# Weight buffers laid at equal places modulo 512 bytes in a hybrid decoder block

## The chip, the cores and the metric

The kernel runs on one core of a Trainium2 chip. The metric is the device time of one execution in microseconds (us), as the median of several runs.

## What is computed

One layer of a decoder block with 256 tokens and D = 2048, all in float32. One projection of the input feeds three branches of width 1024 (gated linear attention A, sliding-window attention B, block attention C). Each branch is projected up to D, weighted by a sigmoid gate, and summed; an output projection, a residual and a LayerNorm follow. Cut to what matters:

```python
def _hybrid_layer(x, w_in, ..., w_branch, w_o, ln_g, ln_b):
    proj = x @ w_in                                  # 2048 x 15632
    ...                                              # ya, yb, yc: three attention branches, each gated
    up = jnp.einsum('bsnw,nwd->bsnd', ys, w_branch)  # 3 x (1024 x 2048)
    gates = jax.nn.sigmoid(mgate.reshape(B, S, N_BRANCH, D) + b_merge)
    merged = jnp.sum(gates * up, axis=2)
    out = merged @ w_o                               # 2048 x 2048
    return _layer_norm(DEEPNORM_ALPHA * x + out, ln_g, ln_b)
```

## The kernel before

**Weights in chunks.** `plan` lists the weight matrices as 324 chunks of 128 x 1024 values (1040 for `av`), in the order of their use (`seq`). `emit_chunk` handles one: SP loads it into a raw buffer (L129, pool `wraw`, four buffers), ACT rounds it to the high part (L130, pool `whi`, three buffers), and DVE subtracts to get the low part (L131, pool `wlo`, three buffers). The buffers of a pool are taken in turn, so chunk number i uses high and low buffer i mod 3. `next_chunk` keeps two chunks ahead of the products. The activations `xhl` (and `ya`, `yb`, `yc`, `mhl`) hold high and low parts too, 512 values per k.

**Two kinds of product.** `mm3` (260 chunks: `aq`, `ak`, `ag`, `bq`, `bkv`, `bg`, `mg`, `wb`, `cq`, `ck`, `cg`) takes the weights as the stationary operand. For each of two column tiles and four k it issues a pair of matmuls; the load of the next weights runs beside the matmul ahead of it:

```python
nc.tensor.matmul(ps, hi[:, k, c], rhs[:, k0 + k, :], ...)                # L236: 512 columns, high part
nc.tensor.matmul(ps[:, 0:S], lo[:, k, c], rhs[:, k0 + k, 0:S], ...)      # L238: 256 columns, low part
```

`nproj` with `nmm` (64 chunks: `av`, `cv`, `wo`) has the activations stationary and the weights moving, in three matmuls per k (L278 to L280).

**Order of the work.** Chunks 0 to 31 are `aq`, `ak` and `av`. Chunks 32 to 131 are `ag`, `bq`, `bkv`, `bg` and the first merge (`mg` and `wb`), with the jobs of branches A and B between them: `tick` issues one step of each job after a chunk's products, so small matmuls and transposes of a job stand between two chunks on TensorE. Chunks 132 to 195 are `cq`, `ck`, `cv` and `cg`, without jobs. Chunks 196 to 213 open the second merge, with the jobs of branch C between them; 214 to 291 are the rest of the second and third merges, without jobs; 292 to 323 are `wo`, and LayerNorm ends the kernel.

**Where the buffers lie.** Pools are laid out one after the other in each partition, in the order of their creation, after the scratch of POOL's own DMA descriptors and the constants. A high or low buffer of 1040 values takes 4160 bytes, 64 more than a multiple of 512, so that three buffers of a pool lie at three places modulo 512:

| Buffers of chunk i | low part, modulo 512 | high part, modulo 512 | moving activations |
|---|---|---|---|
| i mod 3 = 0 | 32 | 224 | 416 |
| i mod 3 = 1 | 160 | 352 | 416 |
| i mod 3 = 2 | 96 | 288 | 416 |

Below, a chunk is said to be of class 0, 1 or 2 by i mod 3.

Of the kernel before, what the change touches and what calls it, by code (L numbers as in the profile page):

```python
# [9 lines left out]
F32 = mybir.dt.float32  # L10
F32R = mybir.dt.float32r
# [6 lines left out]
P = 128  # L18
# [9 lines left out]
RANK = 16  # L28
NV = 260
KC = 4  # L30
NWARM = 8


@with_exitstack
def kernel(ctx: ExitStack, tc: tile.TileContext, xT: bass.AP, x: bass.AP, w_in: bass.AP,
                             w_up: bass.AP, gla_b: bass.AP, norm_g: bass.AP, sinks: bass.AP, b_merge: bass.AP,
                             w_branch: bass.AP, w_o: bass.AP, ln_g: bass.AP, ln_b: bass.AP, out: bass.AP):
    nc = tc.nc

    const = ctx.enter_context(tc.tile_pool(name="const", bufs=1))  # L40
    wraw = ctx.enter_context(tc.tile_pool(name="wraw", bufs=4))
    wlo = ctx.enter_context(tc.tile_pool(name="wlo", bufs=3))
    whi = ctx.enter_context(tc.tile_pool(name="whi", bufs=3))
    acts = ctx.enter_context(tc.tile_pool(name="acts", bufs=1))
    work = ctx.enter_context(tc.tile_pool(name="work", bufs=2))
    pp = ctx.enter_context(tc.tile_pool(name="pp", bufs=2, space=PSUM))
    pa = ctx.enter_context(tc.tile_pool(name="pa", bufs=4, space=PSUM))

    # The weight chunks in the order of their use; loads and splits run ahead of the products.
    seq = []  # L50

    def deep(cols):
# [53 lines left out]
    def emit_chunk():  # L106
        i = state["in"]
        state["in"] += 1
        src, row0, col0, cols, name = seq[i]
        kc = deep(cols)  # L110

        def shaped(t):
            return t.rearrange("p (k c) -> p k c", c=cols)
        raw = shaped(wraw.tile([P, KC * NV], F32, tag="wraw", name=f"w{name}")[:, :kc * cols])
        if name.startswith("wo4_"):
            if not last:
                last["h"] = acts.tile([P, KT, 256], F32R, tag="y", name="wlasth", bufs=2)
                last["l"] = acts.tile([P, KT, 256], F32R, tag="y", name="wlastl", bufs=2)
            k0 = KC * int(name[4:])
            hi, lo = last["h"][:, k0:k0 + KC, :], last["l"][:, k0:k0 + KC, :]  # L120
        else:
            hi = shaped(whi.tile([P, KC * NV], F32R, tag="whi", name=f"h{name}")[:, :kc * cols])
            lo = shaped(wlo.tile([P, KC * NV], F32R, tag="wlo", name=f"l{name}")[:, :kc * cols])
        view = src[row0:row0 + kc * P, col0:col0 + cols].rearrange("(k p) c -> p k c", p=P)
        cuts = [0, 1, 2] if i < 2 else [0, kc]
        for a, b in zip(cuts, cuts[1:]):
            if name.startswith("aq_"):
                load_x(row0 // P + a, row0 // P + b)
            nc.sync.dma_start(raw[:, a:b, :], view[:, a:b, :])  # L129
            nc.scalar.copy(hi[:, a:b, :], raw[:, a:b, :])  # L130
            nc.vector.tensor_tensor(lo[:, a:b, :], raw[:, a:b, :], hi[:, a:b, :].bitcast(F32), op=ALU.subtract)  # L131
        ready.append((name, hi, lo))
# [6 lines left out]
        state["out"] += 1  # L139
        return hi, lo  # L140

    # Side work, cut in steps; one step of each running job is issued between two chunks.
    jobs = []

    def tick():
# [12 lines left out]
    xhl = acts.tile([P, KT, 2 * S], F32R, tag="x", name="xhl")  # L158
    xst = acts.tile([P, KT, S], F32, tag="y", name="xst", bufs=2)

    # The tensor engine's clock rises only while it is busy: keep it so until the first operands are there.
    wz = const.tile([P, 512], mybir.dt.bfloat16, name="wz")
    nc.vector.memset(wz, 0.0)
    pw = pa.tile([P, 512], F32, tag="pa", name="pw")
# [8 lines left out]
    nc.gpsimd.tensor_copy(ones, onesf)  # L173
    onerow = const.tile([P, 1], F32, name="onerow")
    nc.gpsimd.memset(onerow, 1.0)
    # The low-rank gate's weights three times over the rows (high, low, high parts), zeros between.
    wup3 = work.tile([96, 512], F32, tag="r", name="wup3")
    nc.gpsimd.memset(wup3, 0.0)
    for i in range(3):
# [23 lines left out]
    for i in (0, 2):  # L203
        nc.gpsimd.affine_select(mska[:, i, :], mska[:, i, :], pattern=[[-1, P]], compare_op=ALU.is_ge,
                                fill=NEG, base=0, channel_multiplier=1)
    # [row, column]: 1 where column > row; where column >= row; where column < row
    trif = work.tile([P, P], F32, tag="q1", name="trif", bufs=4)
    tril = const.tile([P, P], F32, name="tril")
    triu = const.tile([P, P], F32, name="triu")
# [98 lines left out]
    for k in range(0, KT, 2):  # L308
        hi, lo = next_chunk(f"aq_{k // 2}")
# [16 lines left out]
    def gla_job():  # L326
# [15 lines left out]
            return hl  # L342

        def sums(hl, name):
            # Sums over the partitions, the same in each row.
            pd = pa.tile([P, 512], F32, tag="pa", name=f"pd{name}")
            for e in range(2):
                nc.tensor.matmul(pd, ones, hl[:, e, :], start=e == 0, stop=e == 1)
            return pd
# [165 lines left out]
    def keys_job():  # L515
        nc.gpsimd.dma_start(ksw[0:64, :], bkv[64:128, 0, :])
        nc.gpsimd.dma_start(ksw[64:128, :], bkv[0:64, 0, :])
        yield from wait(2)
        # A key tile's values as [low parts | high parts]
        pv = pa.tile([P, 2, 2, 64], F32, tag="pa", name="pvb")  # L520
        for t in range(2):
            nc.tensor.transpose(pv[:, t, :, :], bkv[:, 1, t * P:(t + 1) * P], ident)
        nc.scalar.copy(vz[:, :, :, 64:P], pv)
        nc.vector.tensor_tensor(vz[:, :, :, 0:64], pv, vz[:, :, :, 64:P].bitcast(F32), op=ALU.subtract)
        yield from wait(2)
        for g in range(2):
            for r in range(2):
                rows = slice(64 * r, 64 * r + 64)
                src = bkv[rows, 0, :] if g == r else ksw[rows, :]
                nc.scalar.copy(ks[rows, g, 0, :], src)  # L530
                nc.vector.tensor_tensor(ks[rows, g, 1, :], src, ks[rows, g, 0, :].bitcast(F32), op=ALU.subtract)
# [1 line left out]
    yb = acts.tile([P, 8, 2 * S], F32R, tag="y", name="yb", bufs=2)  # L533

    def swa_job(hp):
        # A head's queries stand over its 64 rows as their high and low parts: products with the keys' high
        # parts twice and low parts twice give all four terms.
        g = hp // 4
        c0 = 1024 + 512 * (hp % 2)
        qs = swaw[:, c0:c0 + 512].rearrange("p (j c) -> p j c", j=2)  # L540
# [6 lines left out]
        nc.gpsimd.dma_start(qs[0:64, 1, :], ql[64:128, :])  # L547
        yield from wait(4)
        sm = work.tile([P, 2, 2, P], F32, tag="sm", name=f"smb{hp}", bufs=2)
        st = work.tile([P, 12], F32, tag="st", name=f"stb{hp}", bufs=3)  # L550
        nm, den, es = (st[:, 4 * i:4 * i + 4].rearrange("p (j t) -> p j t", j=2) for i in range(3))
        for j in range(2):
            ps = pa.tile([P, 4, P], F32, tag="pa", name=f"sb{hp}{j}")
# [125 lines left out]
    def moba_job(hp):  # L679
        scale = 128.0 ** -0.5  # L680
        sm = work.tile([P, 2, 3 * P], F32, tag="sm", name=f"smc{hp}", bufs=2)
        st = work.tile([P, 12], F32, tag="st", name=f"stc{hp}", bufs=3)
        nm, den = (st[:, 4 * i:4 * i + 4].rearrange("p (t j) -> p t j", t=2) for i in range(2))
        for j in range(2):
            h = 2 * hp + j
            ps = pa.tile([P, 512], F32, tag="pa", name=f"sc{hp}{j}")
            nc.tensor.matmul(ps[:, 0:P], cq[:, h, 0:P], ck[:, h, 0:P], start=True, stop=True)
            nc.tensor.matmul(ps[:, P:3 * P], cq[:, h, P:S], ck[:, h, :], start=True, stop=True)
            nc.vector.scalar_tensor_tensor(sm[:, j, :], ps[:, 0:3 * P], scale,
                                           mska.rearrange("p a b -> p (a b)"), op0=ALU.mult, op1=ALU.add)  # L690
        parts = (slice(0, P), slice(P, 3 * P))
        for t in range(2):
            nc.vector.tensor_reduce(nm[:, t, :], sm[:, :, parts[t]], axis=AX.X, op=ALU.max, negate=True)
        for j in range(2):
            for t in range(2):
                nc.scalar.activation(sm[:, j, parts[t]], sm[:, j, parts[t]], AF.Exp, bias=nm[:, t, j:j + 1],
                                     accum_out=den[:, t, j:j + 1])
        nc.vector.reciprocal(den, den)
        for j in range(2):
            for t in range(2):  # L700
                nc.vector.tensor_scalar(sm[:, j, parts[t]], sm[:, j, parts[t]], den[:, t, j:j + 1], None,
                                        op0=ALU.mult)
        yield 1
        yield 1
        yield 1
        ptb = work.tile([P, 2, 3 * P], F32, tag="ptb", name=f"ptbc{hp}", bufs=1)
        for j in range(2):
            pt = pa.tile([P, 512], F32, tag="pa", name=f"ptc{hp}{j}")
            for b in range(3):
                nc.tensor.transpose(pt[:, b * P:(b + 1) * P], sm[:, j, b * P:(b + 1) * P], ident)  # L710
            nc.scalar.copy(ptb[:, j, :], pt[:, 0:3 * P])
        yield 1
        po = pa.tile([P, 2, S], F32, tag="pa", name=f"oc{hp}")
        for j in range(2):
            vs = slice((2 * hp + j) * P, (2 * hp + j + 1) * P)
            nc.tensor.matmul(po[:, j, :], cv[:, 0, vs], ptb[:, j, 0:S], start=True, stop=False,
                             skip_group_check=True)
            nc.tensor.matmul(po[:, j, P:S], cv[:, 1, vs], ptb[:, j, S:3 * P], start=False, stop=True,
                             skip_group_check=True)
        for j in range(2):  # L720
            h = 2 * hp + j
            to_y(yc, h, po[:, j, :], cgate[:, h, :], f"c{h}")
# [33 lines left out]
        nc.vector.bn_stats(bst[:, t, g, :], hx[t][:, gs])  # L756

    def norm_out(t):
        mv = work.tile([P, 4], F32, tag="mv", name=f"mv{t}")
        nc.vector.bn_aggr(mv[:, 0:2], bst[:, t, :, :])  # L760
        nc.scalar.activation(mv[:, 2:3], mv[:, 1:2], AF.Sqrt, bias=epsl, scale=1.0)
        nc.vector.reciprocal(mv[:, 2:3], mv[:, 2:3])
# [2 lines left out]
        for i, (c0, c1) in enumerate(zip(cuts, cuts[1:])):  # L765
            cs = slice(c0, c1)
            h = hx[t][:, cs]
# [55 lines left out]
```

## Time and profile before

| | before |
|---|---|
| median of 3 runs | 975.08 us (974.85 to 978.05) |
| profiled execution | span 973.3 us from first to last instruction; no other time of it is listed |
| TensorE matmuls, busy | 98% of the span, 5598 matmuls |
| TensorE weight loads, busy | 86% |
| DVE / ACT / POOL, busy | 65% / 51% / 10% |
| DMA | 180.64 MB, 186 GB/s over the span |

How to read it: busy time of TensorE counts overlapping matmuls as one stretch, and the duration of one matmul in the profile reaches over the start of the next one. What a matmul adds to the time is the step from its start to the next start, which the timeline shows. A weight load (PEld) overlaps the matmul before it.

### The profile page before, as it was taken

How to read it: one execution, taken by the hardware profiler on the slowest of the kernel's cores; microseconds unless marked ns; L12 is line 12 of the kernel's file. 1: busy time of each engine (PE TensorE's matmuls, PEld its weight loads, DVE VectorE, ACT ScalarE, POOL GpSimd, SP SyncE). 2: the span in 40 equal slices, each digit the busy share in tenths (PEclk: the TensorE clock that was granted, in tenths of full speed). 3: DMA queues.
4: the chain of work that ended last, by engine and by line, in shares of the span. 5: the costliest groups of instructions: out<-in, count | busy, mean ns of one | idle time of the engine just before them, and what ended most of it. 6: DMA issues, size and time to landing. Idle time of an engine off the chain costs nothing.

```text
span 973.3 us, 14360 instructions
## 1 busy us (share of the span) xinstructions
PE 956.5 (98%) x5598; PEld 841.5 (86%) x5598; DVE 632.6 (65%) x780; ACT 500.6 (51%) x735; POOL 93.6 (10%) x127
## 2 busy tenths in 40 slices
PE   8999999999999999999999999999999999999995
PEld 5899889998888888888888888888888888888885
DVE  6544698758878888855544456665656565585556
ACT  6443574457566666644444445654445454563341
POOL 8100000003112322310000000110000000000003
PEclk9999999999999999999999999999999999999998
DMA  9766666555766666567666666487666666655652
GB/s 301 203 180 192 175 174 173 149 138 152 206 179 183 180 171 185 174 217 195 187 186 190 194 190 179 130 259 217 195 190 185 190 193 194 189 179 187 195 181 87
DMA packets 164052, 180.64 MB, mean 186 GB/s; under 512 B 6048, under 2 KB 150336, under 8 KB 163472
## 3 DMA queue, kind: packets, MB, share of 16 engines
q1 hardware_dynamic: 161552, 174.02, 61.7%
q0 software_dynamic: 2144, 5.51, 1.8%
q8 instruction: 44, 0.72, 0.3%
q10 hardware_dynamic: 288, 0.20, 0.1%
q14 instruction: 24, 0.20, 0.1%
HBM read 176.43 MB, written 2.10 MB: 183 GB/s over the span
## 4 chain that ended last, share of the span: by engine, by line
PE 95%; DVE 3%; DMA 1%; SPq 0%; POOL 0%; issue 0%; ACT 0%; DVEq 0%
PE psmg L236 18%; PE psmg L238 9%; PE pu L236 9%; PE pu L238 4%; PE psbq L236 3%; PE psag L236 3%; PE pscg L236 3%; PE pscq L236 3%; PE psck L236 3%; PE pswo L278 3%; PE pswo L280 3%; PE pswo L279 3%; PE psbg L236 2%; PE psav L278 2%; PE psav L279 2%; PE psav L280 2%
## 5 line engine op out<-in xcount | busy, mean ns | idle before, releaser
L236 PE MATMUL psmg<-xhl,hmg 128*128 128x512 f32 x768 | 269.1, 394 | 0.0
L238 PE MATMUL psmg<-xhl,lmg 128*128 128x256 f32 x768 | 214.5, 279 | 0.0
L131 DVE TENSOR_TENSOR lmg<-wmg,hmg 128x1024 fp32r<-128x1024 f32 x96 | 120.1, 1251 | 79.3 <-ACT hmg L130 79.2
L236 PEld LDWEIGHTS psmg<-xhl,hmg 128*128 128x128 f32 x768 | 144.4, 188 | 30.9
L130 ACT CAST hmg<-wmg 128x1024 fp32r<-128x1024 f32 x96 | 100.6, 1048 | 105.4 <-PE psmg L236 33.4
L238 PEld LDWEIGHTS psmg<-xhl,lmg 128*128 128x128 f32 x768 | 144.5, 188 | 0.1
L131 DVE TENSOR_TENSOR lwb<-wwb,hwb 128x1024 fp32r<-128x1024 f32 x48 | 58.8, 1224 | 40.9 <-ACT hwb L130 40.8
L130 ACT CAST hwb<-wwb 128x1024 fp32r<-128x1024 f32 x48 | 50.2, 1047 | 52.8 <-PE psmg L236 34.8
L131 DVE TENSOR_TENSOR lwo<-wwo,hwo 128x1024 fp32r<-128x1024 f32 x28 | 34.2, 1222 | 27.5 <-ACT hwo L130 27.4
L130 ACT CAST hwo<-wwo 128x1024 fp32r<-128x1024 f32 x28 | 29.4, 1050 | 41.9 <-PE pswo L280 38.5
L278 PE MATMUL pswo<-hwo,mhl 128*128 128x512 f32 (+1 forms) x128 | 47.0, 367 | 0.0
L280 PE MATMUL pswo<-hwo,mhl 128*128 128x512 f32 (+1 forms) x128 | 46.8, 366 | 0.0
L279 PE MATMUL pswo<-lwo,mhl 128*128 128x512 f32 (+1 forms) x128 | 46.8, 365 | 0.0
L236 PE MATMUL psbq<-xhl,hbq 128*128 128x512 f32 x128 | 45.6, 398 | 0.0
L236 PE MATMUL psbg<-xhl,hbg 128*128 128x512 f32 x128 | 45.2, 394 | 0.0
L236 PE MATMUL pu<-ya,hwb 128*128 128x512 f32 x128 | 45.0, 393 | 0.0
L236 PE MATMUL pu<-yb,hwb 128*128 128x512 f32 x128 | 45.0, 394 | 0.0
L236 PE MATMUL psag<-xhl,hag 128*128 128x512 f32 x128 | 44.9, 393 | 0.0
L236 PE MATMUL pu<-yc,hwb 128*128 128x512 f32 x128 | 44.6, 392 | 0.0
L236 PE MATMUL pscg<-xhl,hcg 128*128 128x512 f32 x128 | 44.4, 392 | 0.0
L236 PE MATMUL pscq<-xhl,hcq 128*128 128x512 f32 x128 | 44.4, 392 | 0.0
L236 PE MATMUL psck<-xhl,hck 128*128 128x512 f32 x128 | 44.3, 391 | 0.0
(309 smaller groups left out, 2349.5 us busy)
## 6 DMA issues: line engine op xcount, KB each, us to landing
wmg<-in_w_in_dram SPq DMA_DIRECT2D x96, 512.0 KB, 3.8
wwb<-in_w_branch_dram SPq DMA_DIRECT2D x48, 512.0 KB, 3.5
wwo<-in_w_o_dram SPq DMA_DIRECT2D x32, 512.0 KB, 4.5
wav<-in_w_in_dram SPq DMA_DIRECT2D x16, 520.0 KB, 3.7
wag<-in_w_in_dram SPq DMA_DIRECT2D x16, 512.0 KB, 3.7
wbq<-in_w_in_dram SPq DMA_DIRECT2D x16, 512.0 KB, 3.8
wbg<-in_w_in_dram SPq DMA_DIRECT2D x16, 512.0 KB, 3.7
wcq<-in_w_in_dram SPq DMA_DIRECT2D x16, 512.0 KB, 3.8
```

The source lines that it names most:

```text
L130: nc.scalar.copy(hi[:, a:b, :], raw[:, a:b, :])
L131: nc.vector.tensor_tensor(lo[:, a:b, :], raw[:, a:b, :], hi[:, a:b, :].bitcast(F32), op=ALU.subtract)
L236: nc.tensor.matmul(ps, hi[:, k, c], rhs[:, k0 + k, :], start=first and k == 0, stop=False, skip_group_check=True)
L238: nc.tensor.matmul(ps[:, 0:S], lo[:, k, c], rhs[:, k0 + k, 0:S], start=False, stop=last and k == kc - 1, skip_group_check=True)
L278: nc.tensor.matmul(ps[:, t, :cols], sh, hi[:, k, :], start=kk == 0, stop=False, skip_group_check=True)
L279: nc.tensor.matmul(ps[:, t, :cols], sh, lo[:, k, :], start=False, stop=False, skip_group_check=True)
L280: nc.tensor.matmul(ps[:, t, :cols], sl, hi[:, k, :], start=False, stop=kk == KT - 1, skip_group_check=True)
```

## The change

The high and low buffers grow from 4160 to 4608 bytes, a multiple of 512, so that the three of a pool begin at one place modulo 512. To set which place, the raw buffers grow to 4192 bytes, the small statistics tiles `st` and `mv` get pools of their own, created between and after the weight pools, and the scratch for POOL's DMA descriptors is halved to 8192 bytes per partition, which makes room.

| Buffers | before, modulo 512 | after, modulo 512 |
|---|---|---|
| low parts | 32, 96, 160 | 160, 160, 160 |
| high parts | 224, 288, 352 | 352, 352, 352 |
| `xhl`, `mhl`, `ya`, `yb`, `yc`, `av`, `cv` | 416 | 416 |
| raw | 288, 352, 416, 480 | 288, 384, 480, 64 |

No instruction is added, removed or moved: on all five engines the rows, their operands' shapes and their waits stand in the same order as before. The diff, without lines of comments:

```diff
+RCOLS = KC * NV + 8
+WCOLS = 1152
...
     wraw = ctx.enter_context(tc.tile_pool(name="wraw", bufs=4))
     wlo = ctx.enter_context(tc.tile_pool(name="wlo", bufs=3))
+    stat = ctx.enter_context(tc.tile_pool(name="stat", bufs=3))
     whi = ctx.enter_context(tc.tile_pool(name="whi", bufs=3))
+    mvp = ctx.enter_context(tc.tile_pool(name="mvp", bufs=2))
     acts = ctx.enter_context(tc.tile_pool(name="acts", bufs=1))
...
-        raw = shaped(wraw.tile([P, KC * NV], F32, tag="wraw", name=f"w{name}")[:, :kc * cols])
+        raw = shaped(wraw.tile([P, RCOLS], F32, tag="wraw", name=f"w{name}")[:, :kc * cols])
...
-            hi = shaped(whi.tile([P, KC * NV], F32R, tag="whi", name=f"h{name}")[:, :kc * cols])
-            lo = shaped(wlo.tile([P, KC * NV], F32R, tag="wlo", name=f"l{name}")[:, :kc * cols])
+            hi = shaped(whi.tile([P, WCOLS], F32R, tag="whi", name=f"h{name}")[:, :kc * cols])
+            lo = shaped(wlo.tile([P, WCOLS], F32R, tag="wlo", name=f"l{name}")[:, :kc * cols])
...
-        st = work.tile([P, 12], F32, tag="st", name=f"stb{hp}", bufs=3)
+        st = stat.tile([P, 12], F32, tag="st", name=f"stb{hp}")
...
-        st = work.tile([P, 12], F32, tag="st", name=f"stc{hp}", bufs=3)
+        st = stat.tile([P, 12], F32, tag="st", name=f"stc{hp}")
...
-        mv = work.tile([P, 4], F32, tag="mv", name=f"mv{t}")
+        mv = mvp.tile([P, 4], F32, tag="mv", name=f"mv{t}")
...
-    nc = bacc.Bacc("TRN2", target_bir_lowering=False, num_devices=1)
+    nc = bacc.Bacc("TRN2", target_bir_lowering=False, num_devices=1, dynamic_dma_scratch_size=8192)
```

## Rows read from the trace of the kernel before

**Rows 1.** The page: the span, and TensorE's busy time with its share.

```profile
span 973.3 us, 14360 instructions
PE 956.5 (98%) x5598; PEld 841.5 (86%) x5598; DVE 632.6 (65%) x780; ACT 500.6 (51%) x735; POOL 93.6 (10%) x127
```

**Rows 2.** The page's chain that ended last, by engine.

```profile
PE 95%; DVE 3%; DMA 1%; SPq 0%; POOL 0%; issue 0%; ACT 0%; DVEq 0%
```

**Rows 3.** The page's costliest groups: busy us, mean ns | idle before, releaser.

```profile
L236 PE MATMUL psmg<-xhl,hmg 128*128 128x512 f32 x768 | 269.1, 394 | 0.0
...
L131 DVE TENSOR_TENSOR lmg<-wmg,hmg 128x1024 fp32r<-128x1024 f32 x96 | 120.1, 1251 | 79.3 <-ACT hmg L130 79.2
...
L130 ACT CAST hmg<-wmg 128x1024 fp32r<-128x1024 f32 x96 | 100.6, 1048 | 105.4 <-PE psmg L236 33.4
```

**Rows 4.** Timeline of PE, class-0 chunk 132: start us, duration us, instruction.

```profile
415.14 0.39 PE L236 MATMUL pscq<-xhl,hcq 128*128 128x512 f32 x1
...
416.54 0.40 PE L236 MATMUL pscq<-xhl,hcq 128*128 128x512 f32 x1
...
417.24 0.40 PE L236 MATMUL pscq<-xhl,hcq 128*128 128x512 f32 x1
...
417.94 0.39 PE L236 MATMUL pscq<-xhl,hcq 128*128 128x512 f32 x1
```

**Rows 5.** Timeline of PE, class-1 chunk 133, to the first matmul of chunk 134.

```profile
419.32 0.39 PE L236 MATMUL pscq<-xhl,hcq 128*128 128x512 f32 x1
...
420.00 0.39 PE L236 MATMUL pscq<-xhl,hcq 128*128 128x512 f32 x1
...
420.68 0.39 PE L236 MATMUL pscq<-xhl,hcq 128*128 128x512 f32 x1
```

**Rows 6.** Timeline of PE, the first matmul after class-2 chunk 134.

```profile
423.45 0.40 PE L236 MATMUL pscq<-xhl,hcq 128*128 128x512 f32 x1
```

**Rows 7.** Windows: quiet chunks 214-291, 132-163, 180-195; with jobs 32-131, 196-213.

```profile
core 0: us, PE busy (x) PEld busy (x) DVE busy (x) ACT busy (x) POOL busy (x), PEclk, DMA share, GB/s
655.67:871.65 215.98, 215.98 (x1251) 190.36 (x1249) 130.41 (x135) 108.52 (x137) 1.25 (x2) 1.00 0.65 193
415.14:503.74 88.60, 88.60 (x514) 78.08 (x513) 46.02 (x45) 37.51 (x43) 2.03 (x2) 1.00 0.70 202
548.32:592.66 44.34, 44.34 (x258) 39.07 (x256) 23.22 (x22) 20.74 (x23) 0.00 (x0) 1.00 0.69 191
100.41:415.14 314.73, 313.44 (x1888) 278.06 (x1887) 254.30 (x360) 195.11 (x343) 52.59 (x56) 1.00 0.61 171
592.66:655.67 63.01, 63.01 (x378) 56.21 (x377) 43.85 (x73) 37.74 (x79) 6.14 (x10) 1.00 0.61 185
```

**Rows 8.** Timeline of PE, class-1 chunk 88, right after four transposes of a job.

```profile
278.48 0.60 PE L578 MATMUL ptb<-ident,smb 128*128 128x128 f32 x4
...
280.32 0.40 PE L236 MATMUL psmg<-xhl,hmg 128*128 128x512 f32 x1
...
281.02 0.40 PE L236 MATMUL psmg<-xhl,hmg 128*128 128x512 f32 x1
```

**Rows 9.** Timeline of PE, class-1 chunk 100, also right after four transposes.

```profile
317.00 0.39 PE L236 MATMUL psmg<-xhl,hmg 128*128 128x512 f32 x1
...
317.68 0.39 PE L236 MATMUL psmg<-xhl,hmg 128*128 128x512 f32 x1
```

**Rows 10.** Timeline of PE, first matmul of class-1 chunks 37 and 208, after side work.

```profile
115.29 0.40 PE L236 MATMUL psag<-xhl,hag 128*128 128x512 f32 x1
...
634.36 0.48 PE L236 MATMUL psmg<-xhl,hmg 128*128 128x512 f32 x1
```

**Rows 11.** Timeline of PE, first matmul of chunks 165, 166 and 167 (`cv`).

```profile
506.52 0.40 PE L278 MATMUL pscv<-hcv,xhl 128*128 128x512 f32 x1
...
509.31 0.39 PE L278 MATMUL pscv<-hcv,xhl 128*128 128x512 f32 x1
...
512.09 0.39 PE L278 MATMUL pscv<-hcv,xhl 128*128 128x512 f32 x1
```

## The prediction

> **What bounds the kernel now.** I read the page first. TensorE (PE) is busy for 956.5 of 973.3 us [rows 1], and the chain that ended last is 95% PE [rows 2], so a change counts by what it does to the spacing of the matmuls. The splits of the weights have room: a chunk takes ACT 1.05 us and DVE 1.25 us [rows 3], and PE needs about 2.77 us for it. No row of the page shows the spacing itself: the 394 ns of one matmul [rows 3] overlap the next one. So I went to the timeline of PE, where the start of one matmul to the start of the next is the time that it costs.
>
> 260 of the 324 chunks run through `mm3`: eight pairs of a 512-column matmul (high part, L236) and a 256-column one (low part, L238). Chunk i sits in buffers number i mod 3. In the kernel before, chunks with i mod 3 = 1 have their low part at 160 and their high part at 352 modulo 512, just the places that the change gives to all; 0 has 32 and 224, 2 has 96 and 288. Slices of a chunk lie whole multiples of 512 bytes apart (512 per column tile, 1024 per k), so all its stationary reads begin at one place. **The trace of before thus holds the new layout in every third chunk.**
>
> In a stretch without side work, with the granted clock at 1.00 (the upper level, 2.4 GHz, as in all of [rows 7]), the class-0 chunk starts at 415.14 and the next at 417.94: 2.80 us [rows 4]. The class-1 chunk ends at 420.68: 2.74 us [rows 5]. The class-2 chunk ends at 423.45: 2.77 us [rows 6]. No wait of PE stands in these rows. Inside, two pairs of class 0 take 0.70 us (416.54 to 417.24, [rows 4]) and two of class 1 0.68 (419.32 to 420.00, [rows 5]): 350 against 340 ns a pair. The 20 ns by which 8 x 340 ns falls short of 2.74 us are the first two pairs, in which the matmuls still carry the rhythm of the class-0 chunk ahead. The pattern repeats every three chunks: 126 quiet chunks in three stretches take 215.98 + 88.60 + 44.34 = 348.92 us, 2.77 us each [rows 7].
>
> **Two rhythms.** The same places do not always give 340 ns. A class-1 chunk that began after four transposes holds 0.70 us for two pairs to its end (280.32 to 281.02, [rows 8]); another, also right after transposes, holds 0.68 (317.00 to 317.68, [rows 9]). Going through the timeline, I find 13 class-1 chunks that follow directly on side work of PE, the first at 115.29 and the last at 634.36 [rows 10]: 8 stay at 350 ns a pair, 5 come to 340 within four pairs. Two more, whose first low-part matmul waited for a late split, stay at 350. The other class-1 chunks, some 70 that took over from a product in flow, all reach 340. Once in either rhythm, none leaves it before its end. So far a slow rhythm ended with the chunk, since the next chunk lies elsewhere. After the change every chunk has the same places, and **a rhythm should last until side work or a late split breaks it**, be it for 3 chunks or for 78.
>
> **The change, part by part.**
>
> 1. *Places of the weight parts, `mm3` products.* A chunk in the fast rhythm takes 8 x 340 ns = 2.72 us [rows 5], in the slow one 8 x 350 = 2.80 [rows 8], now 2.77 on average [rows 7]: -0.05 or +0.03 us. What counts is how the 260 divide.
>  - The last quiet stretch, 655.67 to 871.65, has 78 chunks and one entry, the end of the last side job. All fast: 78 x 2.72 = 212.2 us, -3.8 on 215.98. All slow: 218.4, +2.4.
>  - The other two quiet stretches have 48 chunks, 132.9 us: -2.4 if fast, +1.5 if slow. I take the middle, -0.5, as they have one entry each.
>  - The remaining 134 (100 and 18 beside jobs [rows 7], 16 at the start) have an entry every few chunks. At 2.77 each they hold 371.2 us of products: all fast -6.7, all slow +4.0. Taking half of them fast, between the 5 in 13 after side work and the all of 70 in flow: -1.3.
> 2. *Places of the parts, other products.* In the 64 chunks of `nproj` the weights are the moving operand. A class-0 chunk of `cv` takes 2.79 us (506.52 to 509.31) and a class-1 chunk 2.78 (509.31 to 512.09) [rows 11]. I take 0; the bound by this row is 64 x 0.01 = 0.6 us either way.
> 3. *Raw buffers (4192 bytes), `stat` and `mvp`, work tiles at other places.* The same number of buffers, the same order on all engines. ACT and DVE have over 1.4 us spare per chunk [rows 3]: 0, unless splits grew by half. If that cover were gone, PE would wait for splits as it hardly does now.
> 4. *Half the DMA scratch.* It serves POOL's own transfers only, 29 of them. POOL is busy for 1.25 us of the last 216 [rows 7]. No row shows this scratch full. The nearest ones are these idle shares; from them 0, and a loss below 1 us if a transfer of the side jobs were held. A gain is excluded, since nothing waits for the scratch now.
>
> The sum for a fast last stretch: -3.8 - 0.5 - 1.3 = -5.6 us, a span of 967.7. The median of the runs (975.08) stands 1.8 us over the profiled span, and the page lists no other time of that execution; so I forecast **969.5 us**.
>
> **Rivals.**
>
> - *The last stretch falls into the slow rhythm, the rest stays mixed.* +2.4 - 0.5 - 1.3 = +0.6: 975.7 us. For it: 8 of 13 entries after side work. Against it: all 70 entries in flow, and the two latest of the 13, which both slid into 340 after three pairs (the last is in [rows 10]).
> - *Slow rhythm in all quiet stretches, and 3 in 8 fast elsewhere.* This is the one on the other side: +2.4 + 1.5 + 0 = +3.9, 979.0 us. Its place is the first chunk after side work; its price 0.03 us a chunk against the present mean; it decides from where under 3 in 8 of the chunks are fast (0.05 x 3 = 0.03 x 5). The class-0 and class-2 chunks, which now break every slow rhythm, are gone: that speaks for it. For a loss of 2.9 us under a quarter may be fast.
> - *No effect.* If a pair's time came from the buffer's number or its neighbours, not from the place modulo 512, the 2.80, 2.74 and 2.77 would stay: 975.1 us. Against it: slices 512 and 1024 bytes apart in one chunk run alike. The Trainium skill holds that it should come out so (SBUF — State Buffer, "Who interferes with whom"): TensorE has one read port for the moving operand and one for the weights, independent of each other, and never waits on anyone. By that rule the sum would be 0. The spread of 2.74 to 2.80 us by chunk [rows 4 to 6] disagrees with it in this kernel: something at the reads depends on where they lie.
> - *All fast.* -3.8 - 2.4 - 6.7 = -12.9: 962.2 us. It needs every entry to find 340.
>
> **How the numbers follow.** A difference under 0.3% (2.9 us) can't be told from no change here, so the bounds are 972.2 and 978.0. I give a fast last stretch 0.53 (all fast, 0.07, included), the slow last stretch with the rest mixed 0.28, no effect 0.08, the slow rhythm nearly everywhere 0.11. Of the first 0.50 end below 972.2 and 0.03 above, as other stretches may turn slow. The second adds 0.02 below (all else fast), 0.01 above 978.0 and 0.25 between. The third is all between. The fourth is 0.08 above and 0.03 between. Faster 0.52, same 0.39, slower 0.09. Cases of both signs hold the chance, so the likeliest one has its own range, 965 to 972.5. The range of the whole reaches from 963.5, which leaves out all fast, to 977.5, which leaves out most of the slow case.
>
> **What would show it.** Right: on the timeline of PE, chunk starts in the quiet stretches lie 2.72 us apart, in the slow rhythm 2.80, and no longer alternate by threes; long runs of equal chunks change only where side work stands between; the window from the first matmul of chunk 214 to the first of `wo` takes 212.2 or 218.4 us. Wrong: chunks that still alternate by threes (places don't matter), a third spacing that no class-1 chunk shows today, rhythms that flip inside a quiet stretch, or new waits of PE on splits.

## The result and the profile after

The changed kernel takes **964.94 us** (median of 5 runs, 964.69 to 966.3) against 975.08 (5 runs beside it, 974.2 to 978.05). The ratio is 0.9895, 95% interval 0.9882 to 0.9908. The forecast was 969.5, in a range of 963.5 to 977.5: the sign and the range held, and the gain is 10.1 us where 5.6 were forecast. The narrower range of the likeliest case, 965 to 972.5, is missed by 0.06 us. The profiled execution took 964.69 us, with a span of 963.0.

The page of the changed kernel: the span, TensorE's (PE) busy time, the chain that ended last, and three of the costliest groups (busy us, mean ns of one | idle before it). Line numbers have moved by six: L242 and L244 are the high and low matmul of `mm3`, L136 and L137 the two splits.

```profile
span 963.0 us, 14360 instructions
PE 946.2 (98%) x5598; PEld 833.9 (87%) x5598; DVE 633.7 (66%) x780; ACT 500.3 (52%) x735; POOL 93.0 (10%) x127
...
PE 93%; DVE 4%; DMA 1%; issue 1%; ACT 1%; SPq 0%; POOL 0%; DVEq 0%
...
L242 PE MATMUL psmg<-xhl,hmg 128*128 128x512 f32 x768 | 264.6, 391 | 0.0
...
L137 DVE TENSOR_TENSOR lmg<-wmg,hmg 128x1024 fp32r<-128x1024 f32 x96 | 120.2, 1252 | 75.1 <-ACT hmg L136 75.1
...
L136 ACT CAST hmg<-wmg 128x1024 fp32r<-128x1024 f32 x96 | 100.6, 1048 | 100.4 <-PE psmg L242 34.1
```

Beside [rows 1 to 3] this shows what did *not* happen. The splits keep their durations (1252 and 1048 ns against 1251 and 1048) and PE is still 98% busy. It is busy for 10.3 us less with the same 5598 matmuls. No engine took over; the matmuls stand closer together.

The timeline of PE in the changed kernel (start us, duration us): the first matmuls of chunks 133, 134 and 135 of `cq`.

```profile
413.48 0.39 PE L242 MATMUL pscq<-xhl,hcq 128*128 128x512 f32 x1
...
416.20 0.39 PE L242 MATMUL pscq<-xhl,hcq 128*128 128x512 f32 x1
...
418.92 0.39 PE L242 MATMUL pscq<-xhl,hcq 128*128 128x512 f32 x1
```

They lie 2.72 us apart, chunk after chunk, where [rows 4 to 6] had 2.80, 2.74 and 2.77 in turn. One matmul still lasts 0.39 us: its duration says nothing of this, only the steps between starts do.

The windows of the changed kernel, by stretch, in this order: quiet chunks 214 to 291, 132 to 163 and 180 to 195; chunks with jobs, 32 to 131 and 196 to 213; `av`, `cv`, and the first 24 of the 32 chunks of `wo`; and the start with `aq` and `ak`.

```profile
core 0: us, PE busy (x) PEld busy (x) DVE busy (x) ACT busy (x) POOL busy (x), PEclk, DMA share, GB/s
648.61:860.77 212.16, 212.16 (x1250) 187.91 (x1249) 130.19 (x135) 108.44 (x137) 1.31 (x2) 1.00 0.67 196
410.74:497.80 87.06, 87.06 (x514) 77.25 (x513) 46.03 (x45) 37.40 (x42) 2.01 (x2) 1.00 0.71 206
542.81:586.34 43.53, 43.53 (x257) 38.49 (x256) 23.22 (x22) 20.75 (x23) 0.00 (x0) 1.00 0.70 194
98.50:410.74 312.24, 310.50 (x1889) 276.06 (x1887) 254.19 (x360) 195.09 (x343) 52.46 (x56) 1.00 0.62 173
586.34:648.61 62.27, 62.27 (x378) 55.72 (x377) 43.71 (x73) 37.60 (x79) 6.07 (x10) 1.00 0.63 188
52.62:98.50 45.88, 45.88 (x386) 45.88 (x385) 20.44 (x17) 18.90 (x20) 0.00 (x0) 1.00 0.66 187
497.80:542.81 45.01, 45.01 (x195) 36.05 (x194) 20.20 (x17) 18.18 (x18) 0.00 (x0) 1.00 0.66 186
860.77:928.28 67.51, 67.51 (x290) 54.08 (x289) 38.29 (x39) 26.33 (x27) 0.00 (x0) 1.00 0.62 193
0.00:52.62 52.62, 49.36 (x265) 39.71 (x265) 32.97 (x36) 27.30 (x35) 23.50 (x50) 1.00 0.83 252
```

The last four stretches as the kernel before had them (the first five are [rows 7]):

```profile
54.16:100.41 46.25, 46.25 (x387) 46.25 (x385) 20.45 (x17) 18.95 (x20) 0.00 (x0) 1.00 0.66 185
503.74:548.32 44.58, 44.58 (x194) 36.11 (x193) 20.20 (x17) 18.18 (x18) 0.00 (x0) 1.00 0.66 188
871.65:938.53 66.88, 66.88 (x291) 54.15 (x289) 38.14 (x39) 26.20 (x26) 0.00 (x0) 1.00 0.62 195
0.00:54.16 54.16, 50.39 (x265) 40.45 (x265) 31.61 (x36) 27.31 (x35) 23.89 (x50) 1.00 0.81 246
```

| Stretch | before | after | change | forecast |
|---|---|---|---|---|
| quiet, chunks 214 to 291 | 215.98 | 212.16 | -3.82 | -3.8 |
| quiet, 132 to 163 and 180 to 195 | 132.94 | 130.59 | -2.35 | -0.5 |
| with jobs, 32 to 131 and 196 to 213 | 377.74 | 374.51 | -3.23 | } -1.3 |
| start, with chunks 0 to 15 | 54.16 | 52.62 | -1.54 | } |
| `av`, `cv`, first 24 chunks of `wo` | 157.71 | 158.40 | +0.69 | 0 |
| rest (last eight chunks of `wo`, LayerNorm) | 34.77 | 34.72 | -0.05 | 0 |
| span | 973.3 | 963.0 | -10.3 | -5.6 |

The start waits for the first loads, and its length varies from one trace to the next: 53.17 to 54.44 us, 53.7 on average, in the six experiments that keep its distances (e6 to e11). About 1 us of its -1.54 is therefore chance.

### The profile page after: what moved, and what is told of

Its sections match the earlier page's. It is cut to its first block, busy times and chain, and to the rows that moved or that the text cites. A ratio compares the mean times of both kernels' runs of the same rounds, so it can differ in the third digit from the quotient of the medians.

```text
span 963.0 us, 14360 instructions
## 1 busy us (share of the span) xinstructions
PE 946.2 (98%) x5598; PEld 833.9 (87%) x5598; DVE 633.7 (66%) x780; ACT 500.3 (52%) x735; POOL 93.0 (10%) x127
## 4 chain that ended last, share of the span: by engine, by line
PE 93%; DVE 4%; DMA 1%; issue 1%; ACT 1%; SPq 0%; POOL 0%; DVEq 0%
PE psmg L242 18%; PE psmg L244 9%; PE pu L242 9%; PE pu L244 4%; PE psbq L242 3%; PE psag L242 3%; PE pscq L242 3%; PE pscg L242 3%; PE psck L242 3%; PE pswo L285 3%; PE pswo L284 3%; PE pswo L286 3%; PE psav L284 2%; PE psav L285 2%; PE psav L286 2%; PE pscv L285 2%
## 5 line engine op out<-in xcount | busy, mean ns | idle before, releaser
L242 PE MATMUL psmg<-xhl,hmg 128*128 128x512 f32 x768 | 264.6, 391 | 0.0
L244 PE MATMUL psmg<-xhl,lmg 128*128 128x256 f32 x768 | 212.1, 276 | 0.0
L137 DVE TENSOR_TENSOR lmg<-wmg,hmg 128x1024 fp32r<-128x1024 f32 x96 | 120.2, 1252 | 75.1 <-ACT hmg L136 75.1
L242 PEld LDWEIGHTS psmg<-xhl,hmg 128*128 128x128 f32 x768 | 144.2, 188 | 29.2
L136 ACT CAST hmg<-wmg 128x1024 fp32r<-128x1024 f32 x96 | 100.6, 1048 | 100.4 <-PE psmg L242 34.1
L244 PEld LDWEIGHTS psmg<-xhl,lmg 128*128 128x128 f32 x768 | 144.2, 188 | 0.1
L137 DVE TENSOR_TENSOR lwb<-wwb,hwb 128x1024 fp32r<-128x1024 f32 x48 | 58.8, 1225 | 38.7 <-ACT hwb L136 38.6
L136 ACT CAST hwb<-wwb 128x1024 fp32r<-128x1024 f32 x48 | 50.3, 1047 | 50.8 <-PE psmg L242 46.9
L137 DVE TENSOR_TENSOR lwo<-wwo,hwo 128x1024 fp32r<-128x1024 f32 x28 | 34.2, 1222 | 27.9 <-ACT hwo L136 27.9
L136 ACT CAST hwo<-wwo 128x1024 fp32r<-128x1024 f32 x28 | 29.4, 1050 | 42.0 <-PE pswo L286 38.9
L242 PE MATMUL psbq<-xhl,hbq 128*128 128x512 f32 x128 | 45.6, 399 | 0.0
L242 PE MATMUL psbg<-xhl,hbg 128*128 128x512 f32 x128 | 44.7, 393 | 0.0
L242 PE MATMUL psag<-xhl,hag 128*128 128x512 f32 x128 | 44.6, 393 | 0.0
L242 PE MATMUL pu<-yb,hwb 128*128 128x512 f32 x128 | 44.2, 391 | 0.0
L242 PE MATMUL pu<-ya,hwb 128*128 128x512 f32 x128 | 44.2, 390 | 0.0
L242 PE MATMUL pu<-yc,hwb 128*128 128x512 f32 x128 | 43.9, 389 | 0.0
L242 PE MATMUL pscq<-xhl,hcq 128*128 128x512 f32 x128 | 43.6, 389 | 0.0
L242 PE MATMUL pscg<-xhl,hcg 128*128 128x512 f32 x128 | 43.6, 389 | 0.0
L242 PE MATMUL psck<-xhl,hck 128*128 128x512 f32 x128 | 43.6, 389 | 0.0
```

What stands on the lines that cost most here:

```text
L242: nc.tensor.matmul(ps, hi[:, k, c], rhs[:, k0 + k, :], start=first and k == 0, stop=False, skip_group_check=True)
```

## The experiments

The theory: a pair's time hangs on how far the stationary parts (`hi`, `lo`) and the moving activations lie from each other, modulo some power of two. The rivals: the gain came from something else that the change moved (raw buffers, statistics tiles, scratch); only one of the two parts counts; an absolute place counts, not a distance. Unless a diff says otherwise, an experiment is the changed kernel with a `shift` in columns of 4 bytes inside the two enlarged buffers:

```diff
+            oh, ol = shift(i, name)
-            hi = shaped(whi.tile(...)[:, :kc * cols])
-            lo = shaped(wlo.tile(...)[:, :kc * cols])
+            hi = shaped(whi.tile(...)[:, oh:oh + kc * cols])
+            lo = shaped(wlo.tile(...)[:, ol:ol + kc * cols])
```

### e1: the three places of before, in the new buffers

```diff
+        return ((96, 96), (0, 0), (112, 112))[i % 3]
```

> The changed kernel with its buffers, pools and halved scratch, but each chunk's parts shifted inside their buffers so that they turn through the places of before (low 32, 160, 96; high 224, 352, 288 modulo 512). Place theory (the pair's time follows from the places of its weight parts): all of the gain goes; quiet chunks alternate 2.80, 2.74, 2.77 us again, the last quiet stretch takes 216.0 us, time 975 us. Rival (the gain comes from something else in the change: buffer stride, raw buffers, scratch, pools): the last quiet stretch stays at 212.2 us, time 965 us.

Measured: 974.91 us (974.53 to 975.75, 10 runs) against 975.01 for the kernel before; ratio 0.9998 (0.9988 to 1.0007). The window of the last quiet stretch:

```profile
655.91:871.88 215.97, 215.97 (x1250) 190.35 (x1249) 130.36 (x135) 108.55 (x137) 1.25 (x2) 1.00 0.64 193
```

215.97 us against 215.98 before, and the chunks alternate again, 2.80, 2.74 and 2.77 us. Buffers, pools and scratch are the changed kernel's; with the old places alone the whole gain is gone. This shows that the places are the cause, and it prices the raw buffers, the two new pools and the halved scratch at nothing that these runs can tell (-0.1 us, in an interval of about 1 us either way).

### e2 and e5: all chunks at class 0, and the activations moved instead

```diff
# e2
+        return 96, 96
# e5: no shift
-        mv = mvp.tile([P, 4], F32, ...)
+        mv = mvp.tile([P, 24], F32, ...)
```

e2 puts every low part at 32 and every high part at 224. e5 leaves them at 160 and 352 and pushes the pools behind `mvp` along, so that the activations move from 416 to 32 modulo 512.

> All chunks at one place again, but at that of class 0 (low 32, high 224). Place theory: every quiet chunk takes the 2.80 us of class 0, the last quiet stretch 218.4 us; 260 chunks at about 0.08 us over the changed kernel make 982 to 986 us. Rival (equal places as such give the gain, since the rhythm is not upset from chunk to chunk): quiet chunks at 2.72 us, 965 us.

> Weights as in the changed kernel (160 and 352), but the activations moved by 128 bytes, from 416 to 32 modulo 512. Seen from the activations, the weights lie where class 0 had them. Theory that the distance between the stationary and the moving operand counts: as with all chunks at class 0, the last quiet stretch takes 218.4 us, about 982 us. Rival, that only the weights' own place counts: 212.2 us, 965 us.

Measured: e2 982.24 us, ratio 1.0067 (1.005 to 1.0083); e5 982.36 us, ratio 1.0074 (1.0045 to 1.0103). The last quiet stretch of e2, then of e5:

```profile
660.89:879.29 218.40, 218.40 (x1251) 191.95 (x1249) 130.48 (x135) 108.59 (x137) 1.23 (x2) 1.00 0.63 190
```

```profile
661.09:879.49 218.40, 218.40 (x1251) 192.21 (x1249) 130.49 (x135) 108.55 (x137) 1.24 (x2) 1.00 0.62 190
```

218.40 both times: 78 chunks of 2.80 us. e5 did not touch the weights' places, and ACT and DVE write them where they do in the changed kernel; yet it lost the same as e2. In both, the low part begins 128 bytes above the activations modulo 512 (32 against 416, 160 against 32). So the weights' own places do not settle the time, and the distance fits both; whether an absolute place of the activations counts is left to e6. Equal places for all chunks are also no gain by themselves: 17 us lie between the best and the worst of the layouts run so far.

### e6: weights and activations moved together

```diff
# with e5's line
+        return 32, 32
```

> Weights and activations moved together by 128 bytes (low 288, high 480, activations 32 modulo 512). Theory that only distances count: the last quiet stretch takes 212.2 us, 965 us. Rival, that absolute places count (some boundary of 512 bytes): another figure, anywhere between 212 and 220 us.

Measured: 966.28 us, ratio 0.9909 (0.988 to 0.9938). The last quiet stretch:

```profile
650.40:862.56 212.16, 212.16 (x1250) 187.65 (x1249) 130.20 (x135) 108.43 (x137) 1.31 (x2) 1.00 0.64 196
```

212.16 us, as in the changed kernel, though both operands lie elsewhere. The profiled execution is 1.7 us longer than the changed kernel's, and its start alone, at 54.44 us, is 1.8 us longer; 0.6 of that are chunks 8 to 15, which run in the slow rhythm here. The distance is confirmed from the other side, for this one shift of 128 bytes.

### e3 and e4: one part alone

```diff
# e3
+        return 0, (96, 0, 112)[i % 3]
# e4
+        return (96, 0, 112)[i % 3], 0
```

> High parts stay at 352, low parts turn through 32, 160 and 96. Theory that the high part's place alone decides: quiet chunks all at 2.72 us, 965 us. Theory that the low part's place alone decides: 2.80, 2.72, 2.77 us in turn, 973 to 975 us. If both count: between, 967 to 972 us, with the class whose parts lie at 160 and 352 fastest.

> Low parts stay at 160, high parts turn through 224, 352 and 288. Theory that the high part's place alone decides: 2.80, 2.72, 2.77 us in turn, 973 to 975 us. Theory that the low part's place alone decides: all at 2.72 us, 965 us. If both count: between, 967 to 972 us.

Measured: e3 975.22 us, ratio 1.0001 (0.9991 to 1.0011); e4 978.66 us, ratio 1.0038 (1.0026 to 1.005). The last quiet stretch of e3, then of e4:

```profile
655.57:872.06 216.49, 216.49 (x1250) 190.32 (x1249) 130.39 (x135) 108.56 (x137) 1.26 (x2) 1.00 0.64 192
```

```profile
657.21:875.26 218.05, 218.05 (x1251) 191.25 (x1250) 130.53 (x135) 108.55 (x137) 1.23 (x2) 1.00 0.63 191
```

I had thought that half of the change would bring half of the gain. It brings none: setting only the high parts right (e3) gives the old time, setting only the low parts right (e4) costs 0.4% over it. Each part counts, and the two do not add: chunks of e3 take 2.775, 2.732 and 2.820 us by class, so a low part at 96 with a high part at 352 is worse than the old pair 96 and 288 (2.77).

### e7: what starts a slow rhythm

One to four transposes, whose results nothing uses, are put ahead of every sixth chunk of the quiet stretch.

```diff
+        n = state["out"]
+        if n > 214 and n % 6 == 0:
+            pt = pa.tile([P, 512], F32, ...)
+            for t in range(1 + n // 6 % 4):
+                nc.tensor.transpose(pt[:, t * P:(t + 1) * P], ident, ident)
```

> The changed kernel with one to four extra 128x128 transposes on TensorE before every sixth chunk of the last quiet stretch; their results are not used. Theory of two lasting rhythms: each group of six chunks keeps one rhythm, 340 or 350 ns a pair, from its first pairs to its last, some groups fast (16.3 us of products), some slow (16.8 us). By the slow chunks of the profile after (all between chunk 35 and chunk 82) a quarter to a half of the 13 groups are slow. Rival (the rhythm corrects itself after some chunks, or a cause beside TensorE such as the splits sets it): no group stays slow, or rhythms change within a group.

Measured: 972.52 us (one run; before 975.09), span 970.8. Windows of e7 over four chunks each (the second to the fifth) of the groups that begin at chunks 216, 222, 234 and 246, which had one, two, four and two transposes ahead:

```profile
658.06:669.26 11.20, 11.20 (x67) 9.80 (x65) 6.92 (x8) 5.49 (x7) 0.00 (x0) 1.00 0.61 189
675.08:686.28 11.20, 11.20 (x67) 9.80 (x65) 6.80 (x7) 5.48 (x7) 0.00 (x0) 1.00 0.57 178
...
708.93:719.81 10.88, 10.88 (x66) 9.62 (x65) 6.80 (x7) 5.33 (x7) 0.00 (x0) 1.00 0.57 181
...
742.40:753.28 10.88, 10.88 (x66) 9.65 (x65) 5.50 (x5) 5.49 (x7) 0.00 (x0) 1.00 0.62 193
```

Four chunks take 11.20 us (2.80 each) or 10.88 (2.72 each), in one layout, and they differ in what stood ahead of the group. Of 13 groups 7 are slow and 6 fast, and none changes before its last chunk ends (the sixth; the last group has four). With one transpose ahead all four groups are slow, with four all three are fast; with two it goes slow, fast, slow, with three fast, slow, fast. So a rhythm lasts over chunks until something breaks it, as the prediction held. The number of transposes bears on which one starts but does not settle it, and neither does the rhythm ahead: all three groups with two transposes follow a slow group. What does (perhaps the instant at which the first pair falls, within a few ns) stays open.

Of the 7.8 us that the span lost against the changed kernel, 40 slow chunks at 0.08 us are 3.2 and the longer start is 1.1; the other 3.5 are left for 31 transposes and the steps around them.

### e8 and e9: a scan of the distances

Blocks of four to eight chunks get shifts (high, low) of their own, from a table.

> The changed kernel, but blocks of four to six chunks in the quiet stretches and in cv and wo have their parts shifted by chosen distances (high alone, low alone, both). Place theory: each block has a pair time of its own, settled within its first chunk; with both shifted by 128 the pairs take what chunks 128 bytes further from the activations take, none is below 340 ns by much. Rival (340 and 350 are all there is): only these two values appear. In cv and wo, where the weights move and the activations are stationary, the place of the moving operand counts as well: triples between 690 and 710 ns.

> A second scan: the pairs of distances that the first left out for the stationary products, small shifts of 4 to 16 bytes around the changed kernel's places, and for av, cv and wo places around high part + 64 bytes, which took 2.72 us a chunk in wo. Theory that 340 ns a pair is the floor of undisturbed reads: no block is under 2.72 us; all distances other than the changed kernel's (and those 256 bytes from them) are above. Theory that the distance must fit within a few bytes: 4 to 16 bytes already cost, up to the 2.76 us that 32 bytes took. In cv high + 64 gives 2.72 us a chunk against 2.81.

Measured: 972.52 us (e8) and 969.22 us (e9), one run each, of a mixture of layouts. What they are for is the spacing of chunks within each block, read on PE's timeline from chunk start to chunk start once the block has settled. For `mm3`, in us a chunk, by shift from the changed kernel's places:

| shift, bytes | high and low | high alone | low alone |
|---|---|---|---|
| 0 | 2.720 | | |
| 4 | 2.795 | | |
| 8 | | 2.827 | 2.773 |
| 16 | 2.827 | 2.773 | 2.720 |
| 32 | 2.827 | 2.758 | 2.773 |
| 64 | 2.773 | 2.773 | 2.773 |
| 128 | 2.80 | 2.827 | 2.773 |
| 192 | 2.773 | 2.81 to 2.82 | 2.825 |
| 256 | 2.720 | 2.720 | 2.720 |
| 320 | 2.773 | 2.82 to 2.83 | 2.773 |

The shifts of `mm3` blocks that are not in the table (384, 448, 480 and 496, and pairs of two different shifts) lie between 2.77 and 2.83.

Windows of four chunks of e8 at shifts (128, 128), (256, 256), (128, 0) and (256, 0), in this order:

```profile
672.08:683.28 11.20, 11.20 (x66) 9.87 (x65) 5.59 (x6) 5.97 (x8) 0.00 (x0) 1.00 0.61 195
...
705.44:716.32 10.88, 10.88 (x66) 9.65 (x65) 5.78 (x6) 5.97 (x8) 0.00 (x0) 1.00 0.65 203
...
755.16:766.47 11.31, 11.31 (x66) 9.84 (x65) 5.91 (x6) 5.98 (x8) 0.00 (x0) 1.00 0.58 185
...
788.93:799.81 10.88, 10.88 (x67) 9.62 (x65) 5.79 (x6) 5.98 (x8) 0.00 (x0) 1.00 0.66 199
```

And of e9 at (4, 4), (8, 0) and (0, 16):

```profile
785.32:796.50 11.18, 11.18 (x66) 9.79 (x65) 5.86 (x6) 5.98 (x8) 0.00 (x0) 1.00 0.65 202
...
802.13:813.43 11.30, 11.30 (x66) 9.72 (x65) 5.61 (x6) 5.98 (x8) 0.00 (x0) 1.00 0.63 194
...
852.26:863.14 10.88, 10.88 (x66) 9.65 (x65) 8.04 (x11) 8.90 (x14) 0.00 (x0) 1.00 0.57 175
```

e8's rival, that 340 and 350 ns a pair are all there is, is out: these would be 2.72 and 2.80 us a chunk, and blocks settle at 2.758, 2.773 and 2.827 too. e9's floor holds, but two of its guesses fail: 8 bytes on the high part cost more than 32 do, and 16 on the low part cost nothing.

Three things follow. The optimum returns after 256 bytes, not 512, for either part alone and for both. It is narrow: 4 bytes on both parts, or 8 on one, bring back the old mean of 2.77 us a chunk or more. And the changed kernel stands in it: its low parts begin at the activations' place modulo 256 (160 and 416), its high parts 64 bytes below; nothing tried goes under 2.720 us. The old classes are in the table too: class 0 is a shift of 384, that is 128 modulo 256 (2.80), and class 2 is a shift of 448, which e9 measured at 2.773. One entry breaks the pattern: 64 and 320 on the high part alone should be equal and are 2.773 and 2.82. A block is entered once, so an entry can stand for one of two rhythms; that was not taken further.

For the products with the weights as moving operand another distance is best. `cv` takes 2.81 us a chunk at the changed kernel's places and `wo` 2.813; with the high part moved by 64, to the place of the activations, both take 2.720. That is 680 ns for three matmuls, under the 690 to 710 that e8 expected. `av`, whose slices of 260 values lie 1040 bytes apart and so begin at different places, stays between 2.866 and 2.893 at all four shifts tried.

### e10: the best of both

```diff
+        return (16 if name[:3] in ("cv0", "cv1", "wo0", "wo1", "wo2") else 0), 0
```

> The changed kernel with the high parts of the 512-column chunks of cv and wo 64 bytes further on (416, the place of the activations). From the scans 40 chunks at 2.72 us instead of 2.81: cv 43.5 to 43.6 us against 45.0, the last 28 chunks 2.2 us less, in all 3.7 us under the changed kernel: 961.2 us. Rival (the places also upset the chunks that follow): the gain in cv and wo is given back in cg and in the tail, 963 to 965 us.

Measured: **961.33 us** (4 runs, 960.94 to 963.98) against 974.66; ratio 0.9864 (0.9845 to 0.9883), span 959.9. The windows of `cv`, `wo`, the last quiet stretch, and chunks 42 to 45, beside jobs:

```profile
498.39:541.94 43.55, 43.55 (x195) 36.05 (x194) 20.21 (x17) 18.17 (x18) 0.00 (x0) 1.00 0.64 193
859.90:925.21 65.31, 65.31 (x291) 54.08 (x289) 38.29 (x39) 26.31 (x27) 0.00 (x0) 1.00 0.62 200
647.74:859.90 212.16, 212.16 (x1250) 187.65 (x1249) 130.18 (x135) 108.46 (x137) 1.31 (x2) 1.00 0.64 196
128.44:139.64 11.20, 11.20 (x66) 9.80 (x65) 11.20 (x15) 8.31 (x12) 0.00 (x0) 1.00 0.58 177
```

`cv` falls from 45.01 to 43.55 and `wo` from 67.51 to 65.31, 3.66 us together, and the last quiet stretch keeps its 212.16. This version beats the kernel before and the changed one: its slowest run is below the changed kernel's fastest.

### e11: breaking the slow rhythms

Nine chunks from which the 2.80 us rhythm spread in the changed kernel get the worse places, so that the next chunk enters from another spacing.

```diff
# on top of e10
+        if i in (41, 50, 52, 54, 56, 58, 60, 62, 80):
+            return 96, 96
```

> The kernel before this one, and nine chunks that began a slow rhythm in the profile after (41, 50, 52, 54, 56, 58, 60, 62 and 80) laid at the places of class 0. Theory that a chunk at another place breaks the slow rhythm, as every class-0 chunk did before: the chunks behind them (42 to 46, 51, 53 and so on, 81, 82) run at 2.72 to 2.74 us instead of 2.80, the nine themselves stay near 2.80; about 0.9 us less, 960.3 us. Rival (the rhythm is set by the side work and not by the place of the chunk after it): the chunks behind stay at 2.80 us, no change, 961.2 us.

Measured: 961.39 us (4 runs, 961.06 to 961.72), ratio 0.9858 (0.9842 to 0.9875): no difference from e10 that these runs can tell. Windows of e11 over chunks 42 to 45, and 47 and 48:

```profile
128.65:139.55 10.90, 10.90 (x67) 9.63 (x65) 10.90 (x14) 8.04 (x12) 0.00 (x0) 1.00 0.60 179
142.73:148.33 5.60, 5.60 (x34) 4.90 (x32) 5.57 (x6) 2.25 (x3) 0.00 (x0) 1.00 0.70 199
```

The aim was met and the gain was not. Chunks 42 to 45 turned fast, 10.90 us against e10's 11.20. But chunk 46, ahead of a job's matmuls, is now fast, and behind them chunks 47 to 49 came out slow: 47 and 48 take 5.60 us, 5.45 in e10. Together the three lose 0.22 us. Chunks 79 to 82 were slow in the changed kernel's trace, from a late split in 79 on, but were fast in e10's already, so there was nothing to win: they cost 0.15. The stretch of chunks 32 to 131 came to 311.57 us against e10's 311.92, -0.35 where -0.9 was expected.

## Why the prediction was right, and where its sizes were off

**Bound and mechanism: right.** PE bounds both kernels and its spacing is set by the places of the operands. e1 takes the whole gain away by the places alone, e6 keeps it with other places at the same distance. The signs that the prediction named are there: chunk starts 2.72 us apart, no more turn by threes, and 212.16 us in the last stretch, where 212.2 was said for the fast case. One thing the prediction had too narrow: it spoke of the weights' places modulo 512, and the runs show their distance to the activations, modulo 256 (e5, e6, e8, e9). What in the reads makes the distance count, no run shows.

**No effect, the third rival: refuted.** Operands that differ only in where they begin take 2.720 to 2.827 us a chunk, at a granted clock of 1.00 in every window. The Trainium skill (SBUF — State Buffer, "Who interferes with whom") gives TensorE two independent read ports and says that it never waits on anyone; by that the places would not matter. The runs here disagree, as the time hangs on the distance between what the two read.

**The slow last stretch, the first rival: did not happen, but could.** e7 shows the same layout in the slow rhythm in 7 of 13 groups behind transposes. All slow, the stretch would have taken 78 x 2.80 = 218.4 us. In the four traces that keep its layout throughout (the changed kernel, e6, e10, e11) it takes 212.16 each time, so its one entry seems steady. The trace of before could not tell that; with a chance of 0.53 on the fast case, that it came is partly luck.

**The second rival and all fast: neither.** None of the 126 quiet chunks is slow, and 25 others are, which keeps the time above 962.2 us.

**The share of fast chunks: the term that was mis-sized.** For the 48 other quiet chunks I took the middle between all fast and all slow, -0.5; all are fast, and they brought -2.35, the bound of -2.4. For the 134 chunks beside jobs and at the start I took half as fast, -1.3; they brought -4.77. On PE's timeline 25 of them keep the slow rhythm to their end, all between chunks 35 and 82. By the prediction's own terms 109 x 2.72 + 25 x 2.80 = 366.5 us against 371.2, which is -4.7. That this meets -4.77 so closely is luck: apart, the same terms give -3.9 with jobs, where -3.23 was measured, and -0.8 at the start, where -1.54 was. Chunks 41 to 46 are six of the 25, in the changed kernel's timeline below: the first matmuls of chunks 42, 43, 47 and 48, and the two matmuls of a job on L354 that stand ahead of the six and behind them:

```profile
124.29 0.62 PE L354 MATMUL pdd<-hld,ones 128*128 128x512 f32 x2
...
127.54 0.40 PE L242 MATMUL psag<-xhl,hag 128*128 128x512 f32 x1
...
130.34 0.40 PE L242 MATMUL psag<-xhl,hag 128*128 128x512 f32 x1
...
141.54 0.62 PE L354 MATMUL pd<-hl,ones 128*128 128x512 f32 x2
...
142.01 0.39 PE L242 MATMUL psag<-xhl,hag 128*128 128x512 f32 x1
...
144.74 0.39 PE L242 MATMUL psbq<-xhl,hbq 128*128 128x512 f32 x1
```

2.80 us a chunk from 127.54 on, until the job's matmuls at 141.54; the chunk behind them takes 2.73 and is fast. What misled me is that I took the 13 entries of before for a sample of the entries after the change. They are not. In the kernel before, chunks 88, 94, 106, 118 and 130 stay slow behind four transposes, and 100, 112 and 124 come to the fast rhythm ([rows 8, 9] show 88 and 100); the chunk ahead is of class 0 there. In the changed kernel the chunk ahead of these eight is in the fast rhythm, and all eight come to it. Chunk 88 after the change, its four transposes and the first matmuls of its sixth and eighth pair, 0.68 us apart:

```profile
276.11 0.60 PE L584 MATMUL ptb<-ident,smb 128*128 128x128 f32 x4
...
278.26 0.39 PE L242 MATMUL psmg<-xhl,hmg 128*128 128x512 f32 x1
...
278.94 0.39 PE L242 MATMUL psmg<-xhl,hmg 128*128 128x512 f32 x1
```

Of 54 chunks beside jobs that follow directly on side work 45 come to the fast rhythm. The nine slow ones are 35 and 41 behind matmuls on L354, 50, 52, 54, 56, 58 and 60 behind one step of a job (L443), and 62 behind another (L437). The kind of side work does not settle it either: chunk 47, fast above, is slow in e6 behind the same matmuls at the same distances. The window of chunks 47 and 48 of e6:

```profile
143.84:149.44 5.60, 5.60 (x33) 4.89 (x32) 5.57 (x7) 2.26 (x3) 0.00 (x0) 1.00 0.72 210
```

In the six traces that keep the changed kernel's distances in these 134 chunks (its own and e6 to e10), 20 to 32 of them are slow, up to 1 us of difference. So I should have kept the range of that term, not its middle.

**Other products: 0 forecast, +0.69 measured.** The bound of 0.6 was read from two chunks of `cv`. It missed that a chunk between two others at other places does not show the time of its own place: a class-1 chunk of `cv` takes 2.786 to 2.798 us there, but 2.813 when all lie at class 1's places. With all at class 0's (e2) `cv` keeps its 44.58 us. e10 shows that 3.66 us of the changed kernel's time lay here.

**Raw buffers, pools, scratch: 0, confirmed by e1.** Its 974.91 against 975.01 hold all three.

**Of the 4.7 us by which the span's forecast was off**, the quiet chunks make 1.85, the 134 others 3.47 (about 1 of it chance in the start), the other products +0.69 the other way: -1.85 - 3.47 + 0.69 = -4.6, and the rest lies in rounding.

## What to carry to other kernels

Where PE is busy throughout, take the step from one matmul's start to the next from the timeline and compare it between buffers of one pool; a spacing that turns with the buffer's number points at where the operands lie. Then make the buffers a multiple of 256 bytes and scan the distance between stationary and moving operand in steps of a few bytes, for each kind of product apart: here 2.720 and 2.827 us a chunk lay 8 to 16 bytes apart. A layout found this way holds only as long as nothing ahead of it in memory changes size.

## What the runs showed that I had not expected

- A single value of 4 bytes counts: with both parts moved by 4 bytes a chunk takes 2.795 us against 2.720, yet the low part alone may move by 16 at no cost (2.720).
- High and low parts do not add: with the high part right and the low turning, the time of before comes back (975.22 us); with the low part right and the high turning, it is worse (978.66).
- The lowest spacing is the same for stationary and moving weights, 2.720 us for the 6144 columns of a chunk, 0.443 ns a column. Nothing tried went below.
- One layout has two lasting spacings, 2.72 and 2.80 us, and entries that look alike can take either: behind two transposes e7's chunks 222 and 246, and chunk 47 in the changed kernel and in e6. What decides at the entry is not shown.
